# A two-layer hybrid trunk on one core: attention scores of a pair of heads as alternated fp32 matmuls on the two row halves of the array

## The chip, the core and the metric

The kernel runs on one core of a Trainium2 chip. A core has TensorE (PE in the profile; its weight loads are PEld), VectorE (DVE), ScalarE (ACT), GpSimd (POOL) and SyncE (SP, here the queue that issues the DMAs). The metric is device time in microseconds (us) of one execution. PSUM, where PE writes its results, is used in eight banks of 128 x 512 fp32; ACT and DVE empty them.

## The reference

x is (1, 256, 1024), fp32. Two layers of

```
h    = rmsnorm(x, norm_w)
proj = h @ w_in                                   # 1024 x 14368, split into the parts below
A: 16 heads of 64: s = q k^T / 8 + F_q - F_k, causal, softmax, @ v; y_a = o * silu(fg)
B: conv over 4 steps, silu, chunked state-space scan, + d_skip x, * silu(sz), grouped rmsnorm -> y_b
C: 8 heads, two score maps of 64 each after partial rotary on q and k:
   a = softmax(s1) - lam * softmax(s2), @ v (128 wide), rmsnorm; y_c = o * silu(dg)
merged = sum_n sigmoid(mg_n) * (y_n @ w_branch_n)
x      = x + merged @ w_out
```

and a last rmsnorm. Branch A has 16 heads of 64 in its scores and branch C 16 score maps of 64, so a layer has 16 pairs of 64-deep score products, and the kernel 32.

## The kernel before

The 256 tokens are two tiles of 128. Weights come from HBM in chunks of 512 columns, each in four units of 256 rows, by DMA into `raw` (L220). An fp32 weight unit is split into two parts: `whi`, a copy in the format fp32r (ACT, L231), and the remainder `wlo` (DVE, L232). The activations are split in the same way, so that a product is three fp32r matmuls (hi hi, hi lo, lo hi), each one pass on PE. An fp32 matmul, without a split, is two passes, and stands in the trace as two MATMUL records and two LDWEIGHTS.

`bform` (L249) gives a projection with tokens on the partitions, 24 matmuls of 512 columns for a chunk and a token tile; `aform` (L264) gives it with channels on the partitions, 48 matmuls of 256 columns per half of a chunk. Results go to the PSUM pool `pp` (3 banks). Each chunk has an evacuation function; that of fq and fk (branch A) is `t_evac`, that of dq and dk (branch C) is `r_evac` with `rope` behind it. Small work is written as generators (`fox_pair`, `diff_head`, `ssd_x`, `ssd_group`, `transposed`, ...), which `pump` advances between the projections by a budget. From all this a scheduler, which simulates the kernel's timeline while it is built, writes down a fixed order of instructions for each engine; on the chip each engine works through its own order and waits at semaphores.

The score product, before: `split_qk` (L391) makes from a q and k tile (128 partitions, two heads of 64, lower and upper half) operands that stack the parts on 128 rows. `stack_q` (L378) puts q's fp32r part on the rows of its head and the remainder on the other 64 rows (L380 on ACT, L381 on DVE); `stack_k` (L383) puts k's fp32r part on both halves, and the remainder of k likewise into a second tile (L385, L387, L388 on ACT, L386 on DVE). `scores` (L396) then takes one head: for token tile 0 (128 keys) and tile 1 (256 keys), a matmul with k's part (L400) and one with the remainder (L401) into one bank of the pool `pq`. So a pair of heads is eight matmuls. L403 on DVE adds bias and mask and takes the row minimum, L406 on ACT is the exponential. L447 transposes the weights on PE into `pq`, and L457 multiplies by v into a bank of `pt`, fp32, the two heads of branch A on the two column halves.

Three other steps also write to `pt`, and the prediction speaks of them. Each is four transposes of 128x128 (identity as one operand) into one bank:
- `split_rows` (L198): normalised x into `hT`, at the start of a layer, and the merged result; emptied by ACT L188 and DVE L189 in two halves.
- `ssd_x` (L532 before, L516 after): the convolved x of branch B with tokens on the partitions; emptied by DVE L536 and L538 (L520 and L522 after). Its input comes from `conv_tile` (L477), whose last step on DVE is L792 (L778 after).
- `transposed` (L631 before, L615 after): y of the branches B and C, eight blocks of 128 channels in four groups; emptied by ACT L191 and DVE L192, one after the other, for two halves.

`pt` has two banks in the kernel before, `pq` three.

Of the kernel before, what the change touches and what calls it, by code (L numbers as in the profile page):

```python
# [11 lines left out]
F32 = mybir.dt.float32  # L12
F32R = mybir.dt.float32r
# [83 lines left out]
def trunk(ctx: ExitStack, tc: tile.TileContext, x, norm_w, weights, small, vectors,  # L97
# [10 lines left out]
    sm = ctx.enter_context(tc.tile_pool(name="sm", bufs=2))  # L108
    dr = ctx.enter_context(tc.tile_pool(name="dr", bufs=1, space=bass.MemoryType.DRAM))
    pp = ctx.enter_context(tc.tile_pool(name="pp", bufs=3, space=bass.MemoryType.PSUM))  # L110
    pq = ctx.enter_context(tc.tile_pool(name="pq", bufs=3, space=bass.MemoryType.PSUM))
    pt = ctx.enter_context(tc.tile_pool(name="pt", bufs=2, space=bass.MemoryType.PSUM))

    SMALL = nc.sync

# [257 lines left out]

    SPANS = ((0, slice(0, P)), (1, slice(P, 384)))

    LOH, HIH = slice(0, 64), slice(64, P)

    def stack_q(src, dst):  # L378
        for q, main, rest in zip(dst, (LOH, HIH), (HIH, LOH)):
            S.copy(out=q[main], in_=src[main])  # L380
            V.tensor_tensor(out=q[rest], in0=src[main], in1=q[main].bitcast(F32), op=ALU.subtract)  # L381

    def stack_k(src, dst):  # L383
        for k, kl, main, rest in zip(dst[0:2], dst[2:4], (LOH, HIH), (HIH, LOH)):
            S.copy(out=k[main], in_=src[main])  # L385
            V.tensor_tensor(out=kl[main], in0=src[main], in1=k[main].bitcast(F32), op=ALU.subtract)  # L386
            S.copy(out=k[rest], in_=src[main])  # L387
            S.copy(out=kl[rest], in_=kl[main].bitcast(F32))  # L388

    def split_qk(key, src):  # L390
        tiles = [a2(dtype=F32R) for _ in range(2 if key[1] == "q" else 4)]  # L391
        (stack_q if key[1] == "q" else stack_k)(src, tiles)
        return tiles

    def scores(st, pre, b, i, sc, bias, nm, rs):
        j, tk = b % 2, st[f"{pre}k{b // 2}"]  # L396
        q, k, kl = st[f"{pre}q{b // 2}"][i], tk[i], tk[2 + i]
        ps = bank(pq, "pq")
        for o, qs, n in ((0, slice(0, P), P), (P, slice(P, T), T)):
            PE.matmul(ps[:, o:o + n], lhsT=q[:, j, qs], rhs=k[:, j, 0:n], start=True, stop=False)  # L400
            PE.matmul(ps[:, o:o + n], lhsT=q[:, j, qs], rhs=kl[:, j, 0:n], start=False, stop=True)  # L401
        for t, sl in SPANS:
            V.tensor_tensor_reduce(out=sc[:, sl], in0=ps[:, sl], in1=bias[:, sl], scale=-0.125, scalar=BIG,  # L403
                                   op0=ALU.add, op1=ALU.min, accum_out=nm[:, t:t + 1])
        for t, sl in SPANS:
            S.activation(out=sc[:, sl], in_=sc[:, sl], func=AF.Exp, scale=-1.0,  # L406
                         bias=nm[:, t:t + 1], accum_out=rs[:, t:t + 1])

    def fox(l):
        st = L[l]  # L410
# [5 lines left out]
    def fox_pair(l, b, yhi, ylo):  # L416
        st = L[l]
        hb, j = b // 2, b % 2
        yield from need(l, "scr")
        sc = sp.tile([P, 2, 384], F32, name="sc")  # L420
        rows = st["scr"][2 * b:2 * b + 2, :]
        SMALL.dma_start(sc[:, :, 0:P], rows[:, 0:P].partition_broadcast(P))
        SMALL.dma_start(sc[:, :, P:384], rows.partition_broadcast(P))
        for i in (0, 2):
            v = sc[:, :, i * P:(i + 1) * P]
            G.affine_select(out=v, in_=v, pattern=[[0, 2], [-1, P]], compare_op=ALU.is_ge,  # L426
                            fill=NEG, base=0, channel_multiplier=1)
        yield 1, 0.0
        yield from need(l, f"fq{hb}", f"fk{hb}")
        nm = sm.tile([P, 2, 2], F32, name="nm")  # L430
        rs = sm.tile([P, 2, 2], F32, name="rs")
        for i in range(2):
            scores(st, "f", b, i, sc[:, i, :], sc[:, i, :], nm[:, i, :], rs[:, i, :])
        ri = sm.tile([P, 2, 2], F32, name="ri")
        V.reciprocal(out=ri, in_=rs)
        V.tensor_scalar(out=ri, in0=ri, scalar1=0.5, scalar2=None, op0=ALU.mult)
        for i in range(2):
            for t, sl in SPANS:
                V.tensor_scalar(out=sc[:, i, sl], in0=sc[:, i, sl], scalar1=ri[:, i, t:t + 1],
                                scalar2=None, op0=ALU.mult)  # L440
        yield 2, 2.2
        yield from need(l, "fv", f"fg{hb}")
        pTs = []
        for i in range(2):
            ps = bank(pq, "pq")
            for t in range(3):
                PE.transpose(ps[:, t * P:(t + 1) * P], sc[:, i, t * P:(t + 1) * P], ident)  # L447
            pT = tp.tile([P, 384], F32, name="pT", bufs=3)
            done = S.copy(out=pT, in_=ps[:, 0:384]).ins
            pTs.append(pT)  # L450
        yield 1, 0.0
        po = bank(pt, "pt")
        with tc.high_priority(URGENT):
            for t, o, n in ((0, 0, T), (1, P, P)):
                for i in range(2):
                    h = 2 * b + i
                    mm = PE.matmul(po[64 * i:64 * i + 64, o:T],  # L457
                                   lhsT=st["fv"][t][h // 8][:, h % 8 * 64:(h % 8 + 1) * 64],
                                   rhs=pTs[i][:, t * T:t * T + n], start=(t == 0), stop=(t == 1))
                    if t + i == 0:  # L460
                        tc.add_manual_dep(mm.ins, done.name, mybir.DependencyInfo(
                            mybir.DependencyClass.Sync, mybir.DependencyReason.DATA), reason="both heads")
        yt = sc[:, 0, 0:T]
        V.tensor_tensor(out=yt, in0=po[:, 0:T], in1=st[f"fg{hb}"][:, j, :], op=ALU.mult)
        S.copy(out=at(yhi, b), in_=yt)
        V.tensor_tensor(out=at(ylo, b), in0=yt, in1=at(yhi, b).bitcast(F32), op=ALU.subtract)
        st["_yA"][1] += 1
        if st["_yA"][1] == 8:
            st["yA"] = st["_yA"][0]
        yield 1, 0.75  # L470
# [171 lines left out]
    def rope(l, c):  # L642
# [16 lines left out]
        V.tensor_tensor(out=rp, in0=rp, in1=sw, op=ALU.add)  # L659
        for d_, s_ in views:  # L660
            SMALL.dma_start(s_, d_)
        yield 1, 2.4
        for key, src in (("dq", q), ("dk", k)):
            for jj in range(2):
                st[f"{key}{2 * c + jj}"] = split_qk(key, src[jj])
            yield 1, 1.2 if key[1] == "k" else 2.4

    def diff(l):
        L[l]["_d"] = 0
# [3 lines left out]
    def diff_head(l, h):  # L673
        st, pr = L[l], par[l]
        yield from need(l, f"dq{h // 2}", f"dk{h // 2}")
        sc = sp.tile([P, 2, 384], F32, name="sc")
        nm = sm.tile([P, 2, 2], F32, name="dnm")
        rs = sm.tile([P, 2, 2], F32, name="drs")
        for i in range(2):
            scores(st, "d", h, i, sc[:, i, :], bmask, nm[:, i, :], rs[:, i, :])  # L680
        ri = sm.tile([P, 2, 2], F32, name="dri")
        V.reciprocal(out=ri, in_=rs)
        V.tensor_scalar(out=ri[:, 1, :], in0=ri[:, 1, :], scalar1=pr["nlam"], scalar2=None, op0=ALU.mult)
# [37 lines left out]
    def plan(l):  # L721
# [38 lines left out]

        def t_evac(key):
            def f(jj, ps):
                st[f"{key[0:2]}{2 * int(key[2]) + jj}"] = split_qk(key, ps.rearrange("p (a t) -> p a t", t=T))
            return f

        def r_evac(key):
# [257 lines left out]
```

## Time and profile before

| | us |
|---|---|
| median of 3 runs | 946.94 (946.43 to 947.09) |
| the profiled execution | 947.79 |
| its span, first to last instruction | 946.1 |
| PE busy | 933.5 (99%) |
| DVE busy | 700.1 (74%) |
| ACT busy | 598.3 (63%) |
| POOL busy | 38.3 (4%) |

The profile is of one execution. A page gives the busy time of each engine, the span in 40 slices, the chain of work that ended last (followed back from the last instruction, at each step to what released it), and the costliest groups of instructions. A group or a row names the line of the code, the engine, the operation and out<-in by the tiles' names. The timeline lists single instructions or runs of like ones, with the idle time before them and what ended it in brackets, where there was any. The ends of matmul records are modelled, and neighbouring records overlap; the step from one start to the next tells how long PE was taken. "PEclk" and the windows' clock are the granted clock of TensorE as a share of 2.4 GHz.

### The profile page before, as it was taken

The numbers are of one execution on the slowest core, as the hardware profiler recorded it, in microseconds if no ns is written. First come the engines' busy times: TensorE is split into PE (matmuls) and PEld (weight loads), VectorE is DVE, ScalarE is ACT, GpSimd is POOL, SyncE is SP. The second block draws the span as 40 slices with busy tenths as digits, with TensorE's granted clock in tenths as the row PEclk, the third lists the DMA queues.
The fourth block names the chain that finished last, engine by engine and source line by source line (L and its number), as shares of the span: only waits on it lengthen the run. The fifth ranks groups of instructions, "written<-read, shape, count | busy, mean of one in ns | idle before, by whom it ended". The sixth has DMA issues, their size and how long they took to land.

```text
span 946.1 us, 16256 instructions
## 1 busy us (share of the span) xinstructions
PE 933.5 (99%) x5924; PEld 838.7 (89%) x5924; DVE 700.1 (74%) x1434; ACT 598.3 (63%) x1141; POOL 38.3 (4%) x71
## 2 busy tenths in 40 slices
PE   7999999999999999999999999999999999999997
PEld 5999999988898988888889999998889999888885
DVE  5778788988667877864668778789777677787473
ACT  4678786644557868654556869666445596875442
POOL 1001100000000000100000110000000000010000
PEclk7999999999999999999999999999999999999999
DMA  6866634664565655555558674356645455554551
GB/s 238 269 208 198 216 114 154 209 209 140 183 194 179 176 189 171 163 168 196 188 182 267 214 212 141 128 179 214 194 146 199 156 185 188 189 168 162 177 183 44
DMA packets 60319, 172.45 MB, mean 182 GB/s; under 512 B 7312, under 2 KB 15824, under 8 KB 60240
## 3 DMA queue, kind: packets, MB, share of 16 engines
q1 hardware_dynamic: 60240, 171.43, 56.2%
q8 instruction: 46, 0.75, 0.3%
q14 instruction: 33, 0.27, 0.1%
HBM read 167.14 MB, written 2.16 MB: 179 GB/s over the span
## 4 chain that ended last, share of the span: by engine, by line
PE 98%; DMA 1%; DVE 1%; ACT 0%; SPq 0%; issue 0%; POOLq 0%
PE pp L249 51%; PE pp L264 34%; PE pq L400 2%; PE pq L587 1%; PE pq L401 1%; PE pt L457 1%; PE pq L447 1%; DMA raw<-in_weights_dram 1%; PE pt L631 1%; PE pt L198 1%; PE pq L696 1%; PE pq L594 0%; PE pt L704 0%; PE pq L503 0%; PE pt L703 0%; PE pt L702 0%
## 5 line engine op out<-in xcount | busy, mean ns | idle before, releaser
L249 PE MATMUL pp<-whi,a 128*128 128x512 f32 (+1 forms) x1472 | 452.5, 387 | 2.0 <-ACT a L188 1.2
L232 DVE TENSOR_TENSOR wlo<-raw,whi 128x1024 fp32r<-128x1024 f32 (+1 forms) x296 | 349.8, 1193 | 79.3 <-ACT whi L231 75.9
L231 ACT CAST whi<-raw 128x1024 fp32r<-128x1024 f32 (+1 forms) x296 | 301.8, 1027 | 123.9 <-PE pp L249 72.3
L264 PE MATMUL pp<-a,whi 128*128 128x256 f32 x1792 | 332.4, 285 | 0.0
L249 PEld LDWEIGHTS pp<-whi,a 128*128 128x128 f32 x1472 | 273.1, 189 | 55.4 <-ACT a L188 1.7
L264 PEld LDWEIGHTS pp<-a,whi 128*128 128x128 f32 x1792 | 281.3, 191 | 1.3 <-issue 1.0
L249 PE MATMUL pp<-wlo,a 128*128 128x512 f32 (+1 forms) x736 | 281.6, 385 | 0.0
L264 PE MATMUL pp<-a,wlo 128*128 128x256 f32 x896 | 254.5, 284 | 0.0
L264 PEld LDWEIGHTS pp<-a,wlo 128*128 128x128 f32 x896 | 171.5, 191 | 0.8 <-issue 0.8
L249 PEld LDWEIGHTS pp<-wlo,a 128*128 128x128 f32 x736 | 138.9, 189 | 25.8 <-DVE wlo L232 0.5
L183 POOL TENSOR_TENSOR rstd<-rstd,mhalf 128x2 f32<-128x2 f32 (+2 forms) x26 | 18.9, 725 | 743.1 <-DVE rstd L181 722.2
L477 DVE SCALAR_TENSOR_TENSOR a<-sw,pT,a 128x255 f32<-128x255 f32 (+2 forms) x96 | 42.0, 476 | 6.2 <-ACT a L474 6.0
L406 ACT ACTIVATE sc<-sc,dnm 128x128 f32<-128x128 f32 x64 | 28.6, 449 | 8.4 <-DVE dnm L403 8.3
L188 ACT CAST a<-pt 128x256 fp32r<-128x256 f32 x32 | 11.5, 371 | 33.2 <-PE pt L198 26.7
L813 DVE SCALAR_TENSOR_TENSOR a<-a,pp 128x512 f32<-128x512 f32 x24 | 16.4, 682 | 21.0 <-PE pp L249 21.0
L400 PE MATMUL pq<-a,a 128*128 128x128 f32 (+1 forms) x128 | 31.9, 284 | 0.0
L401 PE MATMUL pq<-a,a 128*128 128x128 f32 (+1 forms) x128 | 31.5, 269 | 0.0
L406 ACT ACTIVATE sc<-sc,nm 128x128 f32<-128x128 f32 (+1 forms) x64 | 28.5, 447 | 1.4 <-DVE nm L403 1.2
L426 POOL TENSOR_SCALAR_AFFINE_SELECT sc<-sc 128x256 f32<-128x256 f32 x32 | 17.6, 552 | 159.6 <-DMA sc<-scr 122.8
L400 PEld LDWEIGHTS pq<-a,a 128*128 128x128 f32 x128 | 23.7, 191 | 0.4
L403 DVE CUSTOM_DVE_ANT_0 sc<-pq,sc 128x128 f32<-128x128 f32 (+1 forms) x64 | 19.5, 351 | 6.0 <-POOL sc L426 5.0
L401 PEld LDWEIGHTS pq<-a,a 128*128 128x128 f32 x128 | 23.6, 191 | 0.3
(159 smaller groups left out, 822.2 us busy)
## 6 DMA issues: line engine op xcount, KB each, us to landing
raw<-in_weights_dram SPq DMA_DIRECT2D x280, 512.0 KB, 4.5
raw<-in_weights_dram SPq DMA_DIRECT2D x16, 272.0 KB, 3.5
sc<-scr SPq DMA_DIRECT2D x16, 256.0 KB, 5.9
a<-scr SPq DMA_DIRECT2D x16, 256.0 KB, 5.7
a<-in_x_dram SPq DMA_DIRECT2D x8, 256.0 KB, 5.8
sc<-scr SPq DMA_DIRECT2D x16, 128.0 KB, 5.3
a<-in_norm_w_dram SPq DMA_DIRECT2D x4, 256.0 KB, 6.3
rp<-a SPq DMA_DIRECT2D x32, 32.0 KB, 4.2
```

What stands on the lines that cost most here:

```text
L183: G.tensor_tensor(out=r[:, 0:width], in0=r[:, 0:width], in1=mhalf[:, 0:width], op=ALU.pow)
L231: S.copy(out=hi, in_=raw)
L232: V.tensor_tensor(out=lo, in0=raw, in1=hi.bitcast(F32), op=ALU.subtract)
L249: PE.matmul(ps[:, 0:n], lhsT=at(a, kt)[:, ts], rhs=w[:, k, 0:n], start=((u, k, i) == order[0]), stop=((u, k, i) == order[-1]))
L264: PE.matmul(ps[:, j * T:(j + 1) * T], lhsT=w[:, k, c0:c0 + P], rhs=at(a, kt), start=(kt == 0 and j == 0 and i == 0), stop=(kt == KT - 1 an ...
L400: PE.matmul(ps[:, o:o + n], lhsT=q[:, j, qs], rhs=k[:, j, 0:n], start=True, stop=False)
L401: PE.matmul(ps[:, o:o + n], lhsT=q[:, j, qs], rhs=kl[:, j, 0:n], start=False, stop=True)
L403: V.tensor_tensor_reduce(out=sc[:, sl], in0=ps[:, sl], in1=bias[:, sl], scale=-0.125, scalar=BIG, op0=ALU.add, op1=ALU.min, accum_out=nm[: ...
L406: S.activation(out=sc[:, sl], in_=sc[:, sl], func=AF.Exp, scale=-1.0, bias=nm[:, t:t + 1], accum_out=rs[:, t:t + 1])
L426: G.affine_select(out=v, in_=v, pattern=[[0, 2], [-1, P]], compare_op=ALU.is_ge, fill=NEG, base=0, channel_multiplier=1)
L477: V.scalar_tensor_tensor(out=xc[:, s:T], in0=u[:, 0:T - s], scalar=pr["conv"](j, k), in1=xc[:, s:T], op0=ALU.mult, op1=ALU.add)
L813: V.scalar_tensor_tensor(out=t, in0=t, scalar=1.0, in1=ps, op0=ALU.add, op1=ALU.mult)
```

## The change

q and k are no longer split or stacked: `t_evac` copies the projection into one fp32 tile, and `rope` hands on its fp32 tiles. `scores` now takes a pair of heads: for each token tile, head 0 on array rows 0 to 63 and head 1 on rows 64 to 127, as fp32 matmuls of 64 rows each, alternated, into two banks of `pq`. `pq` gets a fourth bank for it and `pt` is left with one. A first matmul of a pair waits on a POOL instruction (`held`): the mask L426 in branch A, a new memset of one column in branch C. The generators of `rope` yield with other gaps and budgets.

```diff
--- before.py
+++ after.py
@@ -108,8 +108,8 @@
     sm = ctx.enter_context(tc.tile_pool(name="sm", bufs=2))
     dr = ctx.enter_context(tc.tile_pool(name="dr", bufs=1, space=bass.MemoryType.DRAM))
     pp = ctx.enter_context(tc.tile_pool(name="pp", bufs=3, space=bass.MemoryType.PSUM))
-    pq = ctx.enter_context(tc.tile_pool(name="pq", bufs=3, space=bass.MemoryType.PSUM))
-    pt = ctx.enter_context(tc.tile_pool(name="pt", bufs=2, space=bass.MemoryType.PSUM))
+    pq = ctx.enter_context(tc.tile_pool(name="pq", bufs=4, space=bass.MemoryType.PSUM))
+    pt = ctx.enter_context(tc.tile_pool(name="pt", bufs=1, space=bass.MemoryType.PSUM))
 
     SMALL = nc.sync
 
@@ -373,38 +373,23 @@
 
     SPANS = ((0, slice(0, P)), (1, slice(P, 384)))
 
-    LOH, HIH = slice(0, 64), slice(64, P)
-
-    def stack_q(src, dst):
-        for q, main, rest in zip(dst, (LOH, HIH), (HIH, LOH)):
-            S.copy(out=q[main], in_=src[main])
-            V.tensor_tensor(out=q[rest], in0=src[main], in1=q[main].bitcast(F32), op=ALU.subtract)
-
-    def stack_k(src, dst):
-        for k, kl, main, rest in zip(dst[0:2], dst[2:4], (LOH, HIH), (HIH, LOH)):
-            S.copy(out=k[main], in_=src[main])
-            V.tensor_tensor(out=kl[main], in0=src[main], in1=k[main].bitcast(F32), op=ALU.subtract)
-            S.copy(out=k[rest], in_=src[main])
-            S.copy(out=kl[rest], in_=kl[main].bitcast(F32))
-
-    def split_qk(key, src):
-        tiles = [a2(dtype=F32R) for _ in range(2 if key[1] == "q" else 4)]
-        (stack_q if key[1] == "q" else stack_k)(src, tiles)
-        return tiles
-
-    def scores(st, pre, b, i, sc, bias, nm, rs):
-        j, tk = b % 2, st[f"{pre}k{b // 2}"]
-        q, k, kl = st[f"{pre}q{b // 2}"][i], tk[i], tk[2 + i]
-        ps = bank(pq, "pq")
+    def scores(st, pre, b, sc, bias, nm, rs, held):
+        j, q, k = b % 2, st[f"{pre}q{b // 2}"], st[f"{pre}k{b // 2}"]
+        ps = [bank(pq, "pq") for _ in range(2)]
         for o, qs, n in ((0, slice(0, P), P), (P, slice(P, T), T)):
-            PE.matmul(ps[:, o:o + n], lhsT=q[:, j, qs], rhs=k[:, j, 0:n], start=True, stop=False)
-            PE.matmul(ps[:, o:o + n], lhsT=q[:, j, qs], rhs=kl[:, j, 0:n], start=False, stop=True)
-        for t, sl in SPANS:
-            V.tensor_tensor_reduce(out=sc[:, sl], in0=ps[:, sl], in1=bias[:, sl], scale=-0.125, scalar=BIG,
-                                   op0=ALU.add, op1=ALU.min, accum_out=nm[:, t:t + 1])
-        for t, sl in SPANS:
-            S.activation(out=sc[:, sl], in_=sc[:, sl], func=AF.Exp, scale=-1.0,
-                         bias=nm[:, t:t + 1], accum_out=rs[:, t:t + 1])
+            for i in range(2):
+                r = slice(64 * i, 64 * i + 64)
+                mm = PE.matmul(ps[i][:, o:o + n], lhsT=q[r, j, qs], rhs=k[r, j, 0:n], start=True, stop=True)
+                if o + i == 0:
+                    tc.add_manual_dep(mm.ins, held.name, mybir.DependencyInfo(
+                        mybir.DependencyClass.Sync, mybir.DependencyReason.DATA), reason="place for the scores")
+        for i in range(2):
+            for t, sl in SPANS:
+                V.tensor_tensor_reduce(out=sc[:, i, sl], in0=ps[i][:, sl], in1=bias(i)[:, sl], scale=-0.125,
+                                       scalar=BIG, op0=ALU.add, op1=ALU.min, accum_out=nm[:, i, t:t + 1])
+            for t, sl in SPANS:
+                S.activation(out=sc[:, i, sl], in_=sc[:, i, sl], func=AF.Exp, scale=-1.0,
+                             bias=nm[:, i, t:t + 1], accum_out=rs[:, i, t:t + 1])
 
     def fox(l):
         st = L[l]
@@ -423,14 +408,13 @@
         SMALL.dma_start(sc[:, :, P:384], rows.partition_broadcast(P))
         for i in (0, 2):
             v = sc[:, :, i * P:(i + 1) * P]
-            G.affine_select(out=v, in_=v, pattern=[[0, 2], [-1, P]], compare_op=ALU.is_ge,
-                            fill=NEG, base=0, channel_multiplier=1)
+            held = G.affine_select(out=v, in_=v, pattern=[[0, 2], [-1, P]], compare_op=ALU.is_ge,
+                                   fill=NEG, base=0, channel_multiplier=1).ins
         yield 1, 0.0
         yield from need(l, f"fq{hb}", f"fk{hb}")
         nm = sm.tile([P, 2, 2], F32, name="nm")
         rs = sm.tile([P, 2, 2], F32, name="rs")
-        for i in range(2):
-            scores(st, "f", b, i, sc[:, i, :], sc[:, i, :], nm[:, i, :], rs[:, i, :])
+        scores(st, "f", b, sc, lambda i: sc[:, i, :], nm, rs, held)
         ri = sm.tile([P, 2, 2], F32, name="ri")
         V.reciprocal(out=ri, in_=rs)
         V.tensor_scalar(out=ri, in0=ri, scalar1=0.5, scalar2=None, op0=ALU.mult)
@@ -659,11 +643,11 @@
         V.tensor_tensor(out=rp, in0=rp, in1=sw, op=ALU.add)
         for d_, s_ in views:
             SMALL.dma_start(s_, d_)
-        yield 1, 2.4
+        yield 2, 2.4
         for key, src in (("dq", q), ("dk", k)):
             for jj in range(2):
-                st[f"{key}{2 * c + jj}"] = split_qk(key, src[jj])
-            yield 1, 1.2 if key[1] == "k" else 2.4
+                st[f"{key}{2 * c + jj}"] = src[jj]
+        yield 1, 0.0
 
     def diff(l):
         L[l]["_d"] = 0
@@ -674,10 +658,10 @@
         st, pr = L[l], par[l]
         yield from need(l, f"dq{h // 2}", f"dk{h // 2}")
         sc = sp.tile([P, 2, 384], F32, name="sc")
+        held = G.memset(sc[:, 0, 0:1], 0.0).ins
         nm = sm.tile([P, 2, 2], F32, name="dnm")
         rs = sm.tile([P, 2, 2], F32, name="drs")
-        for i in range(2):
-            scores(st, "d", h, i, sc[:, i, :], bmask, nm[:, i, :], rs[:, i, :])
+        scores(st, "d", h, sc, lambda i: bmask, nm, rs, held)
         ri = sm.tile([P, 2, 2], F32, name="dri")
         V.reciprocal(out=ri, in_=rs)
         V.tensor_scalar(out=ri[:, 1, :], in0=ri[:, 1, :], scalar1=pr["nlam"], scalar2=None, op0=ALU.mult)
@@ -760,7 +744,9 @@
 
         def t_evac(key):
             def f(jj, ps):
-                st[f"{key[0:2]}{2 * int(key[2]) + jj}"] = split_qk(key, ps.rearrange("p (a t) -> p a t", t=T))
+                t = a2()
+                S.copy(out=t, in_=ps.rearrange("p (a t) -> p a t", t=T))
+                st[f"{key[0:2]}{2 * int(key[2]) + jj}"] = t
             return f
 
         def r_evac(key):
```

The new order of PE around the transposes of y of branch C, at the end of layer 0 (`pt_` and a number is a bank of the pool `pt` in use for one group; "[waits ...]" names the semaphores of the engines waited for). Before:

```order
L249 MATMUL pp_4874<-whi_4646,a2_154 128x512
L631 MATMUL pt_4832<-ident_87,a2_4470 128x128 [waits DVE_49,PE_49]
L631 MATMUL pt_4832<-ident_87,a2_4471 128x128
L631 MATMUL pt_4832<-ident_87,a2_4470 128x128
L631 MATMUL pt_4832<-ident_87,a2_4471 128x128
L249 MATMUL pp_4874<-whi_4652,a2_151 128x512 [waits Activation_49]
L249 MATMUL pp_4874<-wlo_4653,a2_151 128x512
```

The next group, in the bank `pt_4841`, stands 20 L249 further on. After:

```order
L249 MATMUL pp_4768<-whi_4564,a2_156 128x512
L615 MATMUL pt_4603<-ident_87,a2_4062 128x128 [waits DVE_49]
L615 MATMUL pt_4603<-ident_87,a2_4063 128x128
L615 MATMUL pt_4603<-ident_87,a2_4062 128x128
L615 MATMUL pt_4603<-ident_87,a2_4063 128x128
L615 MATMUL pt_4612<-ident_87,a2_4062 128x128 [waits DVE_49,PE_49]
L615 MATMUL pt_4612<-ident_87,a2_4063 128x128
L615 MATMUL pt_4612<-ident_87,a2_4062 128x128
L615 MATMUL pt_4612<-ident_87,a2_4063 128x128
L615 MATMUL pt_4648<-ident_87,a2_4289 128x128 [waits DVE_49,PE_49]
L615 MATMUL pt_4648<-ident_87,a2_4290 128x128
L615 MATMUL pt_4648<-ident_87,a2_4289 128x128
```

The groups follow one another without a matmul between; the fourth, `pt_4657`, follows in the same way.

The order of DVE around the last conv of the x part of branch B, layer 0 (a2_2448 before, a2_2360 after, is its output). Before:

```order
L576 TENSOR_TENSOR a2_2396<-a2_2396,cb_2207 128x512 [waits Activation_49]
L792 SCALAR_TENSOR_TENSOR a2_2448<-sw_2449,a2_2448 128x512 [waits Activation_49]
L232 TENSOR_TENSOR wlo_2618<-raw_2615,whi_2617 128x1024 [waits DMAHW0_49,Activation_49]
L232 TENSOR_TENSOR wlo_2624<-raw_2621,whi_2623 128x1024 [waits DMAHW1_49,Activation_49]
L232 TENSOR_TENSOR wlo_2630<-raw_2627,whi_2629 128x1024 [waits DMAHW2_49,Activation_49]
L591 TENSOR_TENSOR a2_2374<-a2_2374,pq_2596 128x256 [waits PE_49]
L591 TENSOR_TENSOR a2_2383<-a2_2383,pq_2596 128x256
L536 TENSOR_TENSOR a2_2532<-pt_2534,sc_dt_530 128x512 [waits PE_49]
```

After:

```order
L560 TENSOR_TENSOR a2_2304<-a2_2304,cb_2119 128x512 [waits Activation_49]
L232 TENSOR_TENSOR wlo_2530<-raw_2527,whi_2529 128x1024 [waits DMAHW0_49,Activation_49]
L560 TENSOR_TENSOR a2_2307<-a2_2307,cb_2119 128x512 [waits Activation_49]
L232 TENSOR_TENSOR wlo_2536<-raw_2533,whi_2535 128x1024 [waits DMAHW1_49,Activation_49]
L560 TENSOR_TENSOR a2_2308<-a2_2308,cb_2119 128x512 [waits Activation_49]
L232 TENSOR_TENSOR wlo_2542<-raw_2539,whi_2541 128x1024 [waits DMAHW2_49,Activation_49]
L778 SCALAR_TENSOR_TENSOR a2_2360<-sw_2361,a2_2360 128x512 [waits Activation_49]
L232 TENSOR_TENSOR wlo_2548<-raw_2545,whi_2547 128x1024 [waits DMAHW3_49,Activation_49]
L575 TENSOR_TENSOR a2_2286<-a2_2286,pq_2508 128x256 [waits PE_49]
L575 TENSOR_TENSOR a2_2295<-a2_2295,pq_2508 128x256
L520 TENSOR_TENSOR a2_2444<-pt_2446,sc_dt_530 128x512 [waits PE_49]
L522 TENSOR_TENSOR a2_2445<-pt_2446,br0_364 128x512
```

Three L232 that followed the conv's last step L792 now stand ahead of its counterpart L778, and between L778 and the next bank's L520 there is one L232.

The start, as a difference of PE's order (lines with - are of before, with + of after):

```order
 L198 MATMUL pt<-ident,a_142 128x128 [waits Activation_49]
 L198 MATMUL pt<-ident,a_142 128x128
-L198 MATMUL pt<-ident,a_143 128x128 [waits DVE_49]
-L198 MATMUL pt<-ident,a_143 128x128 x3
 L249 MATMUL pp<-whi,a_149 128x512 [waits Activation_49]
 L249 MATMUL pp<-whi,a_149 128x512
```

and some rows further on:

```order
 L249 MATMUL pp<-whi,a_153 128x512 [waits DVE_49]
 L249 MATMUL pp<-whi,a_153 128x512
+L198 MATMUL pt<-ident,a_143 128x128 [waits DVE_49,PE_49]
+L198 MATMUL pt<-ident,a_143 128x128 x3
 L249 MATMUL pp<-whi,a_150 128x512 [waits Activation_49]
 L249 MATMUL pp<-whi,a_150 128x512
```

The transposes of the second part of x, a_143, stand behind six L249 and not ahead of them.

## Rows read from the trace of the kernel before

**Rows 1.** Page, part 1: engine, busy us (share of the span) xinstructions.
```profile
PE 933.5 (99%) x5924; PEld 838.7 (89%) x5924; DVE 700.1 (74%) x1434; ACT 598.3 (63%) x1141; POOL 38.3 (4%) x71
```

**Rows 2.** Page, part 4: the chain that ended last, by line, with shares of the span.
```profile
PE pp L249 51%; PE pp L264 34%; PE pq L400 2%; PE pq L587 1%; PE pq L401 1%; PE pt L457 1%; PE pq L447 1%; DMA raw<-in_weights_dram 1%; PE pt L631 1%; PE pt L198 1%; PE pq L696 1%; PE pq L594 0%; PE pt L704 0%; PE pq L503 0%; PE pt L703 0%; PE pt L702 0%
```

**Rows 3.** Lines by form: out<-in xcount | busy, mean ns | idle before.
```profile
L388 ACT CAST a<-a 64x512 fp32r<-64x512 f32 x32 | 19.8, 619 | 0.6
```

**Rows 4.** Timeline of PE, 72 us: start us, us, instruction xcount [idle before <-releaser].
```profile
72.01 0.22 PE L400 MATMUL pq<-a,a 128*128 128x128 f32 x1
...
72.94 0.28 PE L264 MATMUL pp<-a,wlo 128*128 128x256 f32 x1
```

**Rows 5.** Timeline of PE, 91 us, the P.V matmuls of a pair.
```profile
91.02 0.28 PE L264 MATMUL pp<-a,whi 128*128 128x256 f32 x1
91.23 0.87 PE L457 MATMUL pt<-pT,a 128*64 128x256 f32 x8
92.03 0.88 PE L447 MATMUL pq<-ident,sc 128*128 128x128 f32 x6
```

**Rows 6.** Timeline of PE, 161 and 210 us: fp32 on the full array.
```profile
160.96 1.06 PE L503 MATMUL pq<-a,a 128*128 128x128 f32 x8
161.77 0.48 PE L264 MATMUL pp<-a,whi 128*128 128x256 f32 x2
...
210.14 1.02 PE L581 MATMUL pt<-a,btok 128*128 128x256 f32 x4
211.08 0.50 PE L249 MATMUL pp<-whi,a 128*128 128x512 f32 x1
```

**Rows 7.** Timeline of all engines, the start.
```profile
9.30 0.66 PE L198 MATMUL pt<-ident,a 128*128 128x128 f32 x4 [0.16 <-DVE a L210]
...
13.12 1.05 PE L249 MATMUL pp<-whi,a 128*128 128x512 f32 x2
...
13.88 1.99 ACT L231 CAST whi<-raw 128x1024 fp32r<-128x1024 f32 x2
14.01 0.42 DVE L189 TENSOR_TENSOR a<-pt,a 128x256 fp32r<-128x256 f32 x1 [0.44 <-ACT a L188]
...
14.98 2.07 PE L249 MATMUL pp<-whi,a 128*128 128x512 f32 x4 [0.80 <-ACT whi L231]
```

**Rows 8.** Windows at the start: us, busy by engine, granted clock, DMA share, GB/s.
```profile
8.50:11.10 2.60, 1.28 (x8) 0.82 (x8) 1.02 (x2) 1.32 (x2) 0.00 (x0) 0.76 1.03 412
...
15.00:20.00 5.00, 5.00 (x12) 3.93 (x13) 4.11 (x7) 4.61 (x12) 0.55 (x1) 0.50 0.64 193
20.00:24.00 4.00, 3.98 (x25) 3.28 (x24) 3.65 (x6) 1.84 (x4) 0.00 (x0) 0.99 0.47 141
```

**Rows 9.** Timeline of all engines, 412 us, transposes of yC.
```profile
411.64 0.60 PE L631 MATMUL pt<-ident,a 128*128 128x128 f32 x4
...
412.00 0.48 PE L249 MATMUL pp<-whi,a 128*128 128x512 f32 x1
...
412.28 0.47 ACT L191 ACTIVATE a<-pt,pT 128x256 fp32r<-128x256 f32 x1 [1.74 <-PE pt L631]
...
413.81 0.48 DVE L192 SCALAR_TENSOR_TENSOR a<-pt,pT,a 128x256 fp32r<-128x256 f32 x1 [0.54 <-ACT a L191]
...
416.65 0.60 PE L631 MATMUL pt<-ident,a 128*128 128x128 f32 x4
```

**Rows 10.** Timeline of all engines, 199 us, last conv and its transposes.
```profile
199.03 0.70 DVE L792 SCALAR_TENSOR_TENSOR a<-sw,a 128x512 f32<-128x512 f32 x1
...
199.64 3.94 DVE L232 TENSOR_TENSOR wlo<-raw,whi 128x1024 fp32r<-128x1024 f32 x3
...
203.69 0.75 DVE L591 TENSOR_TENSOR a<-a,pq 128x256 f32<-128x256 f32 x2
203.78 0.60 PE L532 MATMUL pt<-ident,a 128*128 128x128 f32 x4
...
204.35 0.68 DVE L536 TENSOR_TENSOR a<-pt,sc_dt 128x512 f32<-128x512 f32 x1
```

## The prediction, as it was written before the run

> **What bounds the kernel now.** I read the page first, busy times ahead of the chain. PE is busy 933.5 us of a span of 946.1 us, DVE 74% and ACT 63% of it [rows 1]; the chain that ended last lies for 51% in the weight matmuls L249 and for 34% in L264, and the scores, L400 and L401, are 3% of it [rows 2]. So TensorE is the bound, and it has no holes after the start. Two things follow. Work taken from ACT and DVE is worth nothing unless PE waits for it somewhere, and it doesn't. And any wait that the change puts on PE costs its full length, since nothing on PE makes up for it.
>
> The span is that of one execution of 947.79 us; the median of the runs shown is 946.94, 0.85 lower. I add to 947.79 and take 0.85 off at the end. About 0.2% (1.9 us) is what a measurement of this kernel can tell from no change.
>
> **ACT and DVE.** The change takes away the splitting of q and k: on ACT L380, L385, L387 and L388, of which L388 alone is 19.8 us [rows 3], and on DVE L381 and L386. In their place come 16 plain copies per layer. I cost all this at 0: both engines end their work beside a PE that is never idle. The cover would be gone only where PE waits for DVE, and that place is treated below. The memsets on POOL that `held` needs are behind no wait of PE that I can see: 0, at most 1 us over the kernel.
>
> **The scores on PE.** Before, a pair of heads is eight matmuls from 72.01 to the next L264 at 72.94: 0.93 us [rows 4], 32 pairs, 29.8 us. After, a pair is four fp32 matmuls, each of two passes, so eight records again, on half the rows. No row tile occurs in the trace. The nearest rows are the P·V matmuls L457: fp32 with the same columns (two of 256, two of 128), alternated on the two *column* halves of the array. Their eight records take from 91.23 to 92.03, 0.80 us, and the one before them stood 0.21 us instead of 0.12, so 0.89 with the way in [rows 5]. On the full array fp32 passes take 0.235 us at 256 columns (L581, 0.94 us for four) and 0.101 at 128 (L503, 0.81 for eight) [rows 6], so the same eight records without any overlap are 4 x 0.235 + 4 x 0.101 = 1.34 us, and with perfect overlap 0.67. Column halves thus overlap for the most part.
>
> I take row halves at the column halves' 0.81, plus 0.09 in, and 0.05 out, of which no row tells and which I choose: 0.95 for a pair by itself. By the order, in each layer eight pairs stand two by two back to back (I take 1.62 for two), five alone (0.95 each), and three are broken up: one not alternated (1.40), one not alternated and cut by an L264 (1.95), one alternated with its last matmul standing elsewhere (1.70). That is 4 x 1.62 + 5 x 0.95 + 5.05 = 16.3 us a layer against 14.9: **+2.8 us** in all. Bounds: perfect overlap and no switch gives 32 x 0.67 = 21.4, -8; no overlap of row halves gives 32 x 1.34 and 28 runs x 0.14 in and out, 46.8, +17. I take the value of the column tiles, the nearest row.
>
> The column rows bear on a rule here: L457 shows 0.09 us of extra time ahead of the run. The Trainium skill, "TensorEngine Tiling (Array Packing)", Key Properties, says that a change of tiling mode drains the engine, and the rows agree. The same skill's "TensorE: Matmul & The Clock Gate", Part 3, lets row tiles run side by side with a few ns between their starts; by that alone a pair would be near 0.67, the term -8 and the sum 973 us. No run here shows it yet, and the forecast does not use it.
>
> **One bank less for the transposes.** The larger part is `pt` with one bank. All of L198, L516, L565, L457 and L615 write to it, and the next group of transposes must wait until ACT and DVE have emptied the one before. There are three places where the new order has PE meet this.
>
> *yC (L615).* Before, the four groups of four transposes are spread among L249, one at 411.64, the next at 416.65 [rows 9]. After, the order of PE has the sixteen transposes back to back with no matmul between, each group waiting for DVE. ACT and DVE have nothing else there (seven L191 and eight L192 in a row). An undisturbed group starts at 411.64; ACT and DVE then empty its two halves in turn, ACT first at 412.28, DVE last from 413.81 to 414.29 [rows 9]: 2.65 us, and about 2.70 with the hand-over. PE itself is at it for 0.36 (the next L249 is at 412.00). Three waits of 2.34 are 7.0 us. The L249 behind them needs a bank of `pp` whose evacuation stands behind the last L191 on ACT: I put 1.0 us for it, between 0 and the 2.3 of another round. 8.0 us a layer, **+16 us**; bounds 14 and 19.
>
> *ssd_x (L516).* Before, the last conv ended at 199.03 + 0.70 = 199.73 and its transposes began at 203.78 [rows 10]: 4.05 us of slack. After, three of the L232 that followed that conv on DVE stand ahead of it; three took 3.94 us [rows 10]. The slack is nearly gone, and how late DVE is by then decides: between 0 and 4 us of wait, I take 1.5. Right behind, two transposes wait for the one bank. On DVE one L232 (1.31, a third of the 3.94), two L575 (0.75 together as L591), L520 and L522 (0.68 each, as L536) stand until it is free [rows 10]: 3.4, less some 0.4 for the two transposes that PE still does and for what the DVE rows overlap, 3.0. If PE comes late, the L232 is over, and some 1.7 remain. 4.5 us a layer, **+9 us**; bounds 1.7 and 7 a layer.
>
> *Start (L198).* Before, the two groups of transposes of x stood together, the second at 9.30; ACT emptied both ahead of the cast L231 at 13.88, whose end gave PE the matmul at 14.98 [rows 7]. Now the second group stands behind the first six L249, in the one bank, and ACT still has all its L188 ahead of that L231. PE gets to the transposes at about 14.0 (13.12 and two matmuls of 5.00/12 = 0.42 [rows 7, 8]). From there: four transposes 0.66, L188, L189 and L188 at about 0.4 each, L231 1.0 (half of 1.99), and 0.2 for the hand-overs: 17.0 instead of 14.98, **+2.0 us**. Bounds 0 (if the matmuls between them start earlier too) and 3.
>
> **The clock.** At the start PE stood idle or half busy until 14.98; its granted clock was 0.76 from 8.5 to 11.1, 0.50 from 15 to 20 with PE busy the whole time, and 0.99 only after that [rows 8]. So a gap of that kind costs some 5 us at 1.2 GHz behind it, half of which, 2.5 us, is lost. A yC stall of 8 us with transposes in between is as broken a stretch as the start: 2 x 2.5. An ssd_x stall is shorter; I count half: 2 x 1.25. **+7.5 us**; bounds 0 and 10.
>
> **Sum.** 947.8 + 2.8 (scores) + 16 (yC) + 9 (ssd_x) + 2.0 (start) + 7.5 (clock) = 985.1 in a profiled execution, less 0.85: 984.2 us.
>
> **Rivals.**
> 1. *The row halves run in turn.* Everything as above, but a pair takes 1.34 and its switches: +17 in place of +2.8, about 998 us. For it: no row of this trace shows two row tiles at once. Against it: the column tiles do overlap [rows 5, 6]. 0.12.
> 2. *The gaps are there but the clock holds, and the conv isn't late.* No clock term, ssd_x only the bank's 1.7 a layer: 947.8 + 2.8 + 16 + 3.4 + 2.0 - 0.85 = 971 us. For it: a 4 us slack before, and a lighter DVE. Against it: the clock's row at the start. 0.22.
> 3. *Faster.* The place is again the sixteen transposes of yC. If PE comes to them late, because their inputs (the last diff heads, which hang on DVE and ACT) and not the bank set the time, and the lighter DVE brings these inputs early, the waits on `pt` shrink to little; the score pairs at 0.67 then leave -8 + 2.0 and some 1 us of rests: about 942 us. It decides from the point at which all waits on `pt` together are under 6 us. Against it: the order has no matmul between those groups, and the 2.65 us are evacuations that the change doesn't touch. 0.04.
> 4. *No change that can be measured*: the waits and the gain of the scores cancel; the same as 3 with 6 us of waits, about 947 us. 0.02.
>
> **How the numbers follow.** Forecast 0.60, rivals 0.12, 0.22, 0.04, 0.02. The forecast's own range, from the bounds of ssd_x, clock and start, is about 971 to 994. The range takes in rival 2 with its scores at the lower bound (971 - 10.8 = 960, so nearly) and reaches past the first rival: 962 to 1000. Slower by over 0.2%: 0.60 + 0.12 + 0.22 = 0.94; within 0.2%: 0.02; faster: 0.04.
>
> **What would show it.** The profile after should have four stretches of gaps on PE, two at L615 and two at L516, with waits for DVE of about 2.3 us three times a layer at L615; the granted clock should show a 0.5 stretch behind them; L382 runs should last about 0.95 us to the next L264. Wrong if PE stays at 99% busy: then the one bank costs nothing. A pair of L382 near 1.4 us would be the first rival, near 0.7 perfect overlap; PEclk at 9 through the gaps would be the second.

## The result, and the profile after

The change takes 998.49 us (median of 4 runs, 998.22 to 998.98); the kernel before, in the runs beside it, 947.02. The ratio is 1.0539, 95% interval 1.0526 to 1.0551: 5.4% slower. Forecast were 984.2 us in a range of 962 to 1000, slower.

The profiled execution took 998.98 us, its span is 995.7 us against 946.1. So 49.6 us of the 51.2 are inside the span, and 1.6 lie around it. In the other three runs of the change 2.1 to 2.4 us lie around the span, in runs of the kernel before 1.7, so in those it is 0.4 to 0.7.

Page of the change, part 1 (busy us) and two lines of part 2 (40 slices, busy tenths and granted clock of PE). It answers to [rows 1]:

```profile
PE 952.7 (96%) x5924; PEld 836.6 (84%) x5924; DVE 660.4 (66%) x1370; ACT 531.2 (53%) x1029; POOL 42.4 (4%) x87
...
PE   7999999979999999979999999999899999999697
...
PEclk8999999989999999988999999999799999999799
```

PE is busy longer (952.7 against 933.5 us), in part because matmuls at the slow clock count as busy for longer (the groups at L615 below take 1.0 to 1.1 us instead of 0.6), and yet for a smaller share, 96%. The holes stand in few slices. DVE lost 40 us of work and ACT 67, and the kernel is slower all the same: PE was the bound.

The table of waits of PE: what it waited for, us in total, times, longest. Before, the same table had four lines, 5.7 us together, and no wait on a `pt` bank's evacuation (its one line for matmuls into `pt`, 1.7 us at L198, is for an input, L210). After:

```profile
PE pt L615 <- DVE a L192: 13.2, 6, 2.2
PE pt L516 <- DVE a L522: 5.0, 2, 2.6
PE pt L516 <- DVE a L778: 4.9, 2, 2.4
PE pp L249 <- ACT a L188: 3.5, 3, 2.5
PE pp L249 <- ACT whi L231: 2.3, 1, 2.3
PE pp L249 <- ACT a L742: 2.1, 2, 1.1
PE pq L382 <- POOL sc L411: 2.1, 3, 1.0
...
```

The six waits at L615 (two layers, three each) and two of the four at L516, 18.2 us together, are for the one bank of `pt`. The other two, 4.9 us, are for L778, an input that the order with one bank brings late.

Transposes of y of branch C, layer 0, timeline of all engines (start us, us, engine, instruction, idle before and releaser in brackets). They answer to [rows 9]:

```profile
437.98 0.60 PE L615 MATMUL pt<-ident,a 128*128 128x128 f32 x4
438.62 0.47 ACT L191 ACTIVATE a<-pt,pT 128x256 fp32r<-128x256 f32 x1 [4.48 <-PE pt L615]
...
440.15 0.48 DVE L192 SCALAR_TENSOR_TENSOR a<-pt,pT,a 128x256 fp32r<-128x256 f32 x1 [0.54 <-ACT a L191]
...
440.78 1.00 PE L615 MATMUL pt<-ident,a 128*128 128x128 f32 x4 [2.20 <-DVE a L192]
...
443.98 1.09 PE L615 MATMUL pt<-ident,a 128*128 128x128 f32 x4 [2.20 <-DVE a L192]
...
447.26 1.09 PE L615 MATMUL pt<-ident,a 128*128 128x128 f32 x4 [2.20 <-DVE a L192]
...
449.40 0.80 PE L249 MATMUL pp<-whi,a 128*128 128x512 f32 x1 [1.05 <-ACT a L742]
```

One group goes through as it did before: PE at 437.98, the first of four evacuations at 438.62, the last at 440.15. But now PE has nothing else and starts the second group at 440.78. The first cycle is 2.80 us, against 2.70 forecast; the second and third are 3.20 and 3.28, because the four transposes take 1.0 to 1.1 us instead of 0.6. The clock has fallen (the windows below). And the L249 behind waits another 1.05 us for ACT, whose L742 stands behind L191.

Granted clock around both places in layer 0 (columns: window, length, busy us and records of PE, PEld, DVE, ACT, POOL, then granted clock, DMA share, GB/s). It answers to [rows 8]:

```profile
209.00:216.00 7.00, 1.91 (x10) 1.57 (x10) 5.73 (x10) 0.43 (x1) 0.00 (x0) 0.73 0.83 287
216.00:222.00 6.00, 6.00 (x21) 4.74 (x21) 1.20 (x2) 0.00 (x0) 0.00 (x0) 0.75 0.61 186
222.00:226.00 4.00, 4.00 (x27) 3.67 (x27) 2.61 (x12) 1.61 (x4) 0.00 (x0) 1.00 0.00 0
438.00:449.00 11.00, 3.75 (x17) 2.39 (x15) 3.00 (x7) 3.45 (x8) 0.00 (x0) 0.63 0.02 10
449.00:455.00 6.00, 5.60 (x14) 4.46 (x15) 2.09 (x3) 2.90 (x6) 0.00 (x0) 0.54 0.01 3
455.00:460.00 5.00, 5.00 (x24) 4.11 (x23) 3.68 (x3) 3.48 (x4) 0.00 (x0) 1.00 0.61 190
```

From 449 to 455 PE is busy 5.60 of 6.00 us and runs at 0.54, near the lower of its two levels (1.2 GHz); from 455 on it is at 1.00. It is the same behind the ssd_x waits: from 216 to 222 PE is busy the whole time and the mean clock is 0.75.

The ssd_x transposes of layer 0, timeline of all engines. They answer to [rows 10]:

```profile
207.37 1.89 PE L571 MATMUL pq<-a,a 128*128 128x64 f32 x16
...
210.96 0.68 DVE L778 SCALAR_TENSOR_TENSOR a<-sw,a 128x512 f32<-128x512 f32 x1
...
211.70 0.44 PE L516 MATMUL pt<-ident,a 128*128 128x128 f32 x2 [2.44 <-DVE a L778]
...
213.97 0.68 DVE L522 TENSOR_TENSOR a<-pt,br 128x512 f32<-128x512 f32 x1
...
214.79 1.09 PE L516 MATMUL pt<-ident,a 128*128 128x128 f32 x4 [2.65 <-DVE a L522]
```

L571 begins at 207.37 and its records end at 209.26. Then PE waits 2.44 us for L778, which before was done 4.05 us ahead of its transposes; then 2.65 us more for L522, which frees the bank.

The start, which answers to [rows 7]:

```profile
13.55 0.94 PE L198 MATMUL pt<-ident,a 128*128 128x128 f32 x4
...
15.65 2.00 ACT L231 CAST whi<-raw 128x1024 fp32r<-128x1024 f32 x2
...
16.75 1.41 PE L249 MATMUL pp<-whi,a 128*128 128x512 f32 x4 [2.27 <-ACT whi L231]
...
36.38 0.40 PE L249 MATMUL pp<-whi,a 128*128 128x272 f32 x1 [0.73 <-ACT a L717]
```

The next unit's matmul is at 16.75 instead of 14.98, 1.8 us later. Of the weight matmuls (L249 and L264, counted in PE's order), the 60th of the change is 0.7 us later than before's, the 100th, behind the wait at 36.38, 2.2 us and the 240th 2.3 us.

Scores of branch A, timeline of PE. They answer to [rows 4]:

```profile
69.66 0.93 PE L382 MATMUL pq<-a,a 64*128 64x128 f32 x8 [1.04 <-POOL sc L411]
...
73.68 0.28 PE L264 MATMUL pp<-a,wlo 128*128 128x256 f32 x1
73.89 0.93 PE L382 MATMUL pq<-a,a 64*128 64x128 f32 x8
74.75 0.50 PE L264 MATMUL pp<-a,whi 128*128 128x256 f32 x2
...
112.17 1.58 PE L382 MATMUL pq<-a,a 64*128 64x128 f32 x16
113.69 0.39 PE L264 MATMUL pp<-a,wlo 128*128 128x256 f32 x1
```

A pair alone takes from 73.89 to 74.75, 0.86 us, with 0.21 instead of 0.12 ahead of it; two pairs back to back take 112.17 to 113.69, 1.52. At 69.66 PE waited 1.04 us for the mask on POOL.

### The profile page after: what moved, and what is told of

Read it like the earlier page. It is cut to its first block, busy times and chain, and to the rows that moved or that the text cites. A ratio compares the mean times of both kernels' runs of the same rounds, so it can differ in the third digit from the quotient of the medians.

```text
span 995.7 us, 16080 instructions
## 1 busy us (share of the span) xinstructions
PE 952.7 (96%) x5924; PEld 836.6 (84%) x5924; DVE 660.4 (66%) x1370; ACT 531.2 (53%) x1029; POOL 42.4 (4%) x87
## 4 chain that ended last, share of the span: by engine, by line
PE 85%; issue 7%; DVE 5%; ACT 1%; DMA 1%; POOL 1%; POOLq 0%; SPq 0%; DVEq 0%
PE pp L249 44%; PE pp L264 30%; PE pq L382 3%; DVE wlo L232 1%; PE pt L441 1%; PE pq L431 1%; PE pt L615 1%; PE pq L571 1%; ACT a L191 1%; DVE a L551 1%; DVE a L192 1%; PE pq L680 1%; POOL sc L411 1%; PE pt L198 1%; DVE a L560 0%
## 5 line engine op out<-in xcount | busy, mean ns | idle before, releaser
L249 PE MATMUL pp<-whi,a 128*128 128x512 f32 (+1 forms) x1472 | 458.6, 391 | 8.7 <-ACT a L188 3.5
L232 DVE TENSOR_TENSOR wlo<-raw,whi 128x1024 fp32r<-128x1024 f32 (+1 forms) x296 | 349.9, 1194 | 96.7 <-ACT whi L231 93.5
L231 ACT CAST whi<-raw 128x1024 fp32r<-128x1024 f32 (+1 forms) x296 | 300.7, 1028 | 149.4 <-PE pp L249 77.9
L249 PEld LDWEIGHTS pp<-whi,a 128*128 128x128 f32 x1472 | 275.9, 191 | 64.4 <-ACT a L188 4.4
L264 PE MATMUL pp<-a,whi 128*128 128x256 f32 x1792 | 329.9, 285 | 0.0
L249 PE MATMUL pp<-wlo,a 128*128 128x512 f32 (+1 forms) x736 | 285.4, 390 | 0.0
L264 PEld LDWEIGHTS pp<-a,whi 128*128 128x128 f32 x1792 | 279.9, 191 | 5.3 <-issue 5.0
L264 PE MATMUL pp<-a,wlo 128*128 128x256 f32 x896 | 255.0, 285 | 0.0
L264 PEld LDWEIGHTS pp<-a,wlo 128*128 128x128 f32 x896 | 171.5, 191 | 2.4 <-issue 2.4
L249 PEld LDWEIGHTS pp<-wlo,a 128*128 128x128 f32 x736 | 140.6, 192 | 28.4 <-issue 1.3
L192 DVE SCALAR_TENSOR_TENSOR a<-pt,pT,a 128x256 fp32r<-128x256 f32 x32 | 15.4, 481 | 38.4 <-ACT a L191 38.4
L188 ACT CAST a<-pt 128x256 fp32r<-128x256 f32 x32 | 11.8, 369 | 44.3 <-PE pt L198 39.7
L391 ACT ACTIVATE sc<-sc,nm 128x128 f32<-128x128 f32 x64 | 28.3, 443 | 11.9 <-DVE nm L388 10.8
L382 PE MATMUL pq<-a,a 64*128 64x256 f32 (+1 forms) x256 | 30.7, 344 | 2.1 <-POOL sc L411 2.1
L191 ACT ACTIVATE a<-pt,pT 128x256 fp32r<-128x256 f32 x32 | 15.3, 478 | 32.1 <-PE pt L615 26.7
L388 DVE CUSTOM_DVE_ANT_0 sc<-pq,bmask 128x128 f32<-128x128 f32 x64 | 19.0, 353 | 12.2 <-PE pq L382 12.2
L382 PEld LDWEIGHTS pq<-a,a 64*128 64x128 f32 x256 | 19.1, 186 | 8.6 <-issue 3.2
L189 DVE TENSOR_TENSOR a<-pt,a 128x256 fp32r<-128x256 f32 x32 | 13.4, 419 | 19.0 <-ACT a L188 19.0
```

Of the source, the lines that this page charges most:

```text
L191: S.activation(out=hi, in_=ps, func=AF.Copy, scale=scale)
L192: V.scalar_tensor_tensor(out=lo, in0=ps, scalar=scale, in1=hi.bitcast(F32), op0=ALU.mult, op1=ALU.subtract)
L231: S.copy(out=hi, in_=raw)
L232: V.tensor_tensor(out=lo, in0=raw, in1=hi.bitcast(F32), op=ALU.subtract)
L249: PE.matmul(ps[:, 0:n], lhsT=at(a, kt)[:, ts], rhs=w[:, k, 0:n], start=((u, k, i) == order[0]), stop=((u, k, i) == order[-1]))
L264: PE.matmul(ps[:, j * T:(j + 1) * T], lhsT=w[:, k, c0:c0 + P], rhs=at(a, kt), start=(kt == 0 and j == 0 and i == 0), stop=(kt == KT - 1 an ...
```

## The experiments

All times are medians of runs beside runs of the kernel before (947.6 to 948.0 us in these; 947.0 beside the change, so a difference from the change's 998.49 is good to about 1 us).

**e1, one bank in the kernel before.**

```diff
-    pq = ... tile_pool(name="pq", bufs=3, ...)
-    pt = ... tile_pool(name="pt", bufs=2, ...)
+    pq = ... tile_pool(name="pq", bufs=4, ...)
+    pt = ... tile_pool(name="pt", bufs=1, ...)
```

> The kernel before with one bank in pt and four in pq, nothing else; the scores stay fp32r on stacked operands. Theory A (the one bank makes nearly all of the loss, through waits at the yC and ssd_x transposes and the start, and the clock behind them): of the 51.5 us some 46 are there, about 990 us (980 to 996), with waits of PE for L192 of about 13 us. Theory B (the row tiles and the new order of the scores, with less work on ACT and DVE, make it): under 955 us.

Measured: 997.78 us, ratio 1.0529 (1.0514 to 1.0543). The kernel with the old scores and one bank is as slow as the change, and slower than the 980 to 996 us that I expected. Its waits ahead of matmuls into `pt`, but for 0.8 us at L198, which are for an input:

```profile
PE pt L631 <- DVE a L192: 13.2, 6, 2.2
PE pt L631 <- DVE a L711: 5.1, 2, 2.5
PE pt L532 <- DVE a L538: 5.0, 2, 2.6
PE pt L532 <- DVE a L792: 4.9, 2, 2.4
```

L631 and L532 wait as L615 and L516 do in the change, to 0.1 us. There is one more place, yC's first group behind the P·V bank (L711), 5.1 us, which the change does not have and I did not expect. Without it e1 would be at some 993 us, and the change pays about as much for its scores; that the two kernels come out within 1 us of each other is chance. Theory A holds in its mechanism: moving the bank makes a loss of nearly the whole size, with the same waits. Theory B falls.

**e2, two banks in the change.**

```diff
-    pq = ... tile_pool(name="pq", bufs=4, ...)
-    pt = ... tile_pool(name="pt", bufs=1, ...)
+    pq = ... tile_pool(name="pq", bufs=3, ...)
+    pt = ... tile_pool(name="pt", bufs=2, ...)
```

> The change with two banks in pt and three in pq as before; everything else of the change stays. Theory A: the loss is gone but for the scores' own cost and the POOL waits, 952 us (948 to 957). Theory B: still above 975 us.

Measured: 963.43 us, ratio 1.0165 (1.0151 to 1.0179). 35 of the 51 us are gone, and with them all waits on the evacuation of `pt`; the one line of the table of waits that is left for matmuls into `pt` is for an input of L198:

```profile
PE pt L198 <- DVE a L210: 2.1, 2, 1.2
```

The slow stretches are gone too: the mean granted clock of the span is 0.993, against 0.992 to 0.997 in the runs of the kernel before and 0.971 to 0.975 in those of the change. But it is 11 us above what I expected. With three banks in `pq` a second pair finds one bank only, and the scheduler places one head's matmuls alone: 36 runs of row-tile matmuls instead of 28. Timeline of PE, one head:

```profile
68.64 0.92 PE L382 MATMUL pq<-a,a 64*128 64x128 f32 x4
69.49 0.50 PE L264 MATMUL pp<-a,whi 128*128 128x256 f32 x2
```

Its four records take 0.85 us to the next L264, as long as the eight of a pair. Summed over the kernel by the steps from one start to the next, L382 takes 35.9 us, against 28.7 in the change and 29.1 for L400 and L401 before; the steps of L264, which hold the way into a run and the POOL waits, are 6.4 us more than before. So the fourth bank is what the row tiles need, and `pt` is where it was taken from.

**e3, no wait on POOL.**

```diff
-                if o + i == 0:
-                    tc.add_manual_dep(mm.ins, held.name, ...)
-        held = G.memset(sc[:, 0, 0:1], 0.0).ins
+        held = None
```

> The change with one bank in pt, without the wait of the scores on POOL (the dependency on held and the memset are left out). If the POOL waits of PE (2.1 us by the table of waits) and the score runs cut in two cost what the steps before L382 show: 998.5 - 2.6 - some 2 for fewer runs, about 994 us (991 to 996). Rival: that time is given back at the next wait for a bank, which comes anyway: 998 us.

Measured: 993.96 us, ratio 1.0487 (1.0473 to 1.0502), as expected. The wait of L382 on POOL is gone from the table of waits, and in PE's order 20 runs stand in place of 28, twelve of them two pairs. The yC and ssd_x waits are the same to 0.1 us.

**e4, the yC gaps filled.**

```diff
+                    if name == "yC" and i + tt == 0 and fill:
+                        follow(mm, fill[-1])
+            if name == "yC" and j2 < 3:
+                scrap = bank(pq, "pq")
+                fill = [mm]
+                for f in range(NFILL):
+                    fill.append(PE.transpose(scrap[:, f % 4 * P:(f % 4 + 1) * P], ident, ident))
+                    follow(fill[-1], fill[-2])
```

`NFILL` is 18, `follow` puts its first instruction behind its second in the order, and `mm` is the transpose of the group that was written last. Not shown are the lines that define these.

> The change, with 18 transposes of the identity into a bank of pq behind each of the first three groups of the yC transposes, so that PE works through most of each 2.2 us wait; nothing reads them. Theory A with the clock as a term of its own: the granted clock stays at 1.00 through the yC transposes, the slow transposes (some 0.4 us a group) and the half-speed matmuls behind (2.3 and 1.1 us) go, and about 6 us are saved: 992 us (990 to 995). Rival (the waits alone make the loss there): no gain, 998 us or more.

Measured: 992.19 us, ratio 1.0464 (1.0449 to 1.0478): 6 to 7 us less than the change, though PE has 108 transposes more and the groups wait for the same bank. Timeline of PE, one filled gap, and the windows of the clock:

```profile
440.00 2.13 PE L629 MATMUL pq<-ident 128*128 128x128 f32 x18
442.37 0.63 PE L622 MATMUL pt<-ident,a 128*128 128x128 f32 x4 [0.24 <-DVE a L192]
442.83 2.13 PE L629 MATMUL pq<-ident 128*128 128x128 f32 x18
```

```profile
438.00:449.00 11.00, 9.94 (x78) 8.75 (x76) 2.90 (x6) 3.15 (x7) 0.00 (x0) 1.00 0.13 45
449.00:455.00 6.00, 5.30 (x23) 4.39 (x24) 3.33 (x4) 4.96 (x8) 0.00 (x0) 1.00 0.03 5
```

The stretch between two groups is still 2.4 us long, but PE is at work in it, its wait is down to 0.24 us, and the clock stays at 1.00 in both windows where the change had 0.63 and 0.54. The next group starts 2.80 to 2.84 us after the one before in every cycle of both layers. So the clock is a cost of its own in that place, 6 to 7 us in two layers.

**e5, the transposes in the banks of `pq`, no wait on POOL.** One bank in `pt` and four in `pq` as in the change. `split_rows`, `ssd_x` and `transposed` each get the line below, and the scores do without the dependency on `held`, as in e3.

```diff
-        ps = bank(pt, "pt")
+        ps = bank(pq, "pq")
```

> The change with one bank in pt and four in pq, but the transposes of split_rows, ssd_x and transposed go into the four banks of pq, and the scores don't wait for held. Theory A (waits on the one bank, and POOL): all waits and slow stretches go, and twelve of twenty score runs are doubles at 1.51 + 0.19 us, with the shorter runs some 14.8 us a layer against 14.55 + 0.12 a run before: 947 to 950 us. Rival (the loss would only move to the banks of pq, which the scores need two at a time): over 955 us.

Measured: 952.24 us, ratio 1.0047 (1.0034 to 1.0061). It is 46 us faster than the change and 4.6 us slower than the kernel before: a little above the 947 to 950 that I expected and under the rival's 955. Two pairs in a run, and the wait that is left at yC:

```profile
62.20 1.58 PE L382 MATMUL pq<-a,a 64*128 64x128 f32 x16
63.72 0.39 PE L264 MATMUL pp<-a,wlo 128*128 128x256 f32 x1
```

```profile
PE pp L249 <- ACT a L739: 2.1, 2, 1.1
```

L382 takes 26.3 us here, 2.8 less than L400 and L401 before. The runs' way in and out takes it back: the steps of L264 are 2.1 us more, and other runs stand among L249, whose steps are 3.4 us more. Behind the last yC group PE still waits 1.05 us a layer for an evacuation of `pp` that stands behind L191 on ACT; with the transposes of y that is 2.6 us of the difference, by the steps.

**e6, the heads in turn.** As e5, with the loop over heads outside the one over token tiles.

> As e5, but the two matmuls of head 0 stand before the two of head 1 (the loops over heads and token tiles exchanged). If row halves overlap only where neighbours stand on different halves, a pair goes from some 0.67 to 0.76 toward 1.34 us: 6 to 20 us more than e5. If the array overlaps them in any order: the same as e5 within 2 us.

Measured: 956.10 us, ratio 1.0086 (1.0072 to 1.0099). The test did not do what it was made for: in a run of two pairs most records still start in twos, as they do where the heads alternate, and only the last few stand by themselves. Such a run takes 1.61 instead of 1.51 us, 1.2 us for twelve. The spans of the two profiled executions differ by 1.8 us, the medians by 3.9; what makes up the rest I leave open. How row halves overlap is read better from e2's single head.

**e7, two banks in `pp`.** pp 2, pq 4, pt 2, without the wait on POOL.

> The change with two banks in pp, four in pq and two in pt, and without the wait on held. If a projection's bank is emptied well within the 5.4 us that the next tile's 24 matmuls take, nothing waits on pp, and the time is that of e5 with a few more cut runs: 948 to 952 us. Rival: PE waits for pp at the ends of tiles, over 960 us.

Measured: 955.89 us, ratio 1.0091 (1.0077 to 1.0104), between the two cases. PE waits for `pp` only among the first projections (1.9 us, for ACT L714, in two waits). There are 24 runs of scores instead of 20, and two waits of 2.1 us in all for the last conv.

No version beat the kernel before; e5 comes nearest.

## Why the prediction was right, point by point

The direction, the places, and the waits on the bank with the clock behind them came out as forecast. The number is 14.3 us short: 998.49 lies above 971 to 994, the range that the forecast had by its own bounds (worked out again from the bounds of ssd_x, clock and start, it is 969 to 993). It falls inside 962 to 1000 only because that range was stretched past the first rival, which e2's single head refutes, so that part is luck. Term by term below, three were too small: the clock (some 12 to 14 us against 7.5), the scores (5.7 against 2.8) and the boundary of the layers (2.4, not foreseen).

- **The bank (yC).** Right in mechanism and place: 13.2 us of waits at L615 against three times 2.34 a layer, 14.0. From the first L615 to the 30th L249 behind the last is 12.5 us more than 16 x 0.09 + 30 x 0.227 in layer 0 and 11.1 in layer 1, 23.6 with the clock. Forecast were 16 + 5 = 21. What was short is that the clock falls within the stall: the transposes of the later groups ran at the slow clock too and lengthened the cycle from 2.80 to 3.28 us. e1 shows the same waits without the new scores, and e4 the cycle of 2.8 us with the clock held up. Beyond the waits (13.2, and 2.1 for L742) 8.3 us of the 23.6 are left; 6 to 7 of them are the clock by e4, against 5 forecast.
- **ssd_x.** Waits 4.9 and 5.0 us over two layers, 9.9 against a forecast of 9. Its two parts miss in opposite ways: the late input costs 4.9 us and not 3, the bank 5.0 and not 6. The clock term there was mis-sized. I counted half of 2.5 us because the stall was shorter; by the lateness of the same weight matmul before and after (5.1 us at the 1141st, 12.4 at the 1381st; 29.2 at the 3601st and 37.7 at the 3781st, in layer 1) the place costs 7.3 and 8.5 us a layer, 15.8, against 9 + 2.5. So the clock costs some 6 us there and not 2.5. Its slow stretch is in the trace (216 to 222 at 0.75).
- **The start.** 2.3 us against 2.0, but only at first by the chain that was named. That chain made the matmul behind L231 1.8 us late. At the 60th weight matmul 0.7 of it is left, and it grows to 2.2 by the 100th, where PE waits 0.73 us for L717, of which the prediction says nothing. That the sum comes so near is in part luck.
- **The scores.** The pair alone costs 0.86 + 0.09 ahead + 0.10 behind: 1.05 against 0.95; two pairs 1.52 + 0.19 = 1.71 against 1.62. With 28 runs: L382 -0.4 us, and L264 +4.6, of which the POOL waits are 2.1 by the table of waits. 4.2 us in place of 2.8. To it belong the runs among L249, ten with 0.32 instead of 0.23 us ahead and six with 0.34 instead of 0.23 behind, by the steps: another 1.5 us. The way out, of which no row told, is twice what I chose. The POOL waits, put at no more than 1, are 2.1, and they are for the mask of branch A (L411), where the prediction thought of the memsets alone. That row halves overlap as column halves do is confirmed: one head alone takes 0.85 us and two take 0.86, and the records of the two heads start less than 0.02 us apart. The first rival (in turn, 998 us) comes to the right time by a wrong cause.
- **Not foreseen.** At the boundary of the layers L198 stands in four groups on one bank, and the first L249 behind two of them waits for L188 (0.50 and 0.46 us); around there the change falls back 2.4 us. What lies around the span, 1.6 us in the profiled execution, nothing here explains.
- **ACT and DVE relief at 0.** Right: 67 and 40 us less busy and no gain on PE. The plain copies are 16 in the kernel, eight a layer, and not 16 a layer; at a cost of 0 that changes nothing.

Together 23.6 + 15.8 + 2.3 + 4.2 + 2.4 = 48.3 of the 49.6 us in the span; the 1.5 us of score runs among L249 cover what is left. The sum is not exact to tenths, since small work stands in other places of the two orders.

On the two rules that were weighed: the Trainium skill, "TensorEngine Tiling (Array Packing)", Key Properties, has a change of mode drain the engine. The trace agrees, with 0.09 us ahead of a run of row tiles and 0.10 behind it, paid per run, so that the count of runs matters beside the matmuls in them. The Trainium skill, "TensorE: Matmul & The Clock Gate", Part 3, lets row tiles run side by side. The trace agrees, 0.86 us for two heads where one takes 0.85; but the short run never got to 0.67 a pair. The second pair in a run does, at 1.52 - 0.86 = 0.66.

## What to carry to other kernels

What a PSUM bank is worth depends on the order of the instructions: before moving one from a pool to another, look in the new order for groups that follow one another on the pool that lost it. With TensorE as the bound, each such group cost nearly its whole evacuation chain here (2.2 us of wait for a chain of 2.65), and two or three waits in a row cost the clock behind them as well. In the one place where it was tried, with the waits left in, work that nobody reads kept TensorE's clock up and was worth more than it cost (6 to 7 us).

## What was not expected of the hardware

A head's four matmul records on one row half take 0.85 us alone, and the eight records of two heads on both halves 0.86: a row tile that runs by itself gains nothing, and its partner costs 0.01 us. In layer 0 the clock fell within a stall of three 2.2 us waits and stayed low for some 5 us of full work behind it (0.54 from 449 to 455); with 18 transposes that nobody reads in each of those waits it stayed at 1.00 there.
